# The tail of an encoder layer on one core: last columns' sums added to the residual ahead, last products in two halves, one more block weighed on GpSimd

## The chip, the cores and the metric

The kernel runs on one core of a Trainium2 chip. A core has a matrix engine (TensorE; PE in the profile, with PEld for the loads of its stationary operand), a vector engine (VectorE, DVE), a scalar engine (ScalarE, ACT), a general engine (GpSimd, POOL), a synchronizing engine (SyncE, SP) that issues most transfers, and 16 DMA engines. The metric is the time of one execution on the device in microseconds (us); of several runs the median stands.

## The reference

One layer of a streaming encoder for 256 rows of 2048 columns: a half-step feed-forward part, a pooling and gated linear attention mixer, cross attention on 256 memory tokens, a second half-step feed-forward part, and a last norm. Only the end matters here:

```python
D_MODEL, SEQ, D_FF, RMS_EPS = 2048, 256, 5632, 1e-6

def rms_norm(x, gain):
    y = x * lax.rsqrt(jnp.mean(x * x, axis=-1, keepdims=True) + RMS_EPS)
    return y * gain

def swiglu(h, w_gate, w_up, w_down):
    return (jax.nn.silu(h @ w_gate) * (h @ w_up)) @ w_down

x = x + 0.5 * swiglu(rms_norm(x, ffn2_norm), ffn2_w_gate, ffn2_w_up, ffn2_w_down)
out = rms_norm(x, final_norm)
```

## The kernel before

Matrix products keep fp32 accuracy by splitting each operand into a high and a low part and adding three products: high by high, high by low, low by high (`products`, L357). Activations are the stationary operand, 128x128; weights stream past, 512 columns at a time, into one PSUM bank. The 256 rows are two halves h of 128 rows, here called the first rows (h = 0) and the second rows (h = 1). The 2048 columns are four blocks `nb` of 512; two blocks come with one weight unit (b = 0 for blocks 0 and 1, b = 1 for 2 and 3). Weights pass as units of 1 MB: loaded, split by ScalarE and VectorE, then used (`Stream`, L34); an item that `st.op` adds stands in the program's order behind the unit before it. Instructions are issued from each engine's own queue in order. The order within a queue is the scheduler's, except where `in_order` (L1552) keeps the program's, or `issue_after` sets one instruction behind another.

The end of the kernel is the third part of the last down projection (`down_last` and `down_end`, L1486 and L1502). `block_s` (L514) sums most of its inner dimension. For b = 0 the sums go into the residual x at once. For b = 1 they stay in PSUM (`more=True`), because the last two slices of the inner dimension are added to the same banks later. The last two slices are two more units (`end_unit`, L1522), taken in this order:

1. the first rows of blocks 0 and 1, then 2 and 3. For each block come its six products in `mm` (L1507), then `update` (L1535, VectorE: x += 0.5 * sums), `square` (L1541, ScalarE: squares, with their sum per row into `ss`) and `weigh` (L1546, GpSimd: x times the last gain `gB`, written over the scratch of the squares);
2. `second_half` (L1603): the products of the second rows, blocks 0 to 3, and after them in program order the updates, squares and `weigh` of these, `row_factor` (L1555) for each half, and `finish` (L1585), which multiplies a stretch of columns by the row factor `Rcol` and stores it.

Blocks 0 and 1 of the last slices have fresh banks (`pe` in the profile); blocks 2 and 3 go on in `block_s`'s (`pt`). GpSimd weighs all four blocks of the first rows and blocks 0 and 1 of the second. For blocks 2 and 3 of the second rows `finish` multiplies by factor and gain in one VectorE instruction (L1594). Elsewhere it is a ScalarE scale (L1592) or a VectorE `tensor_scalar_mul` (L1598) of the weighed block. `row_factor` takes the sum of squares (for the second rows: the sum of blocks 0 to 2, made ahead by `three_of_four`, plus block 3's), a square root on ScalarE (L1568), and on VectorE a reciprocal, a Newton step and a reciprocal (L1571 to L1575). Its argument `between` is work put on VectorE between the root's issue and the first reciprocal. There are nine stores to `out`; eight are issued on SP, and one (second rows, blocks 0 and 1, 512 KB) on ScalarE's queue.

Of the kernel before, what the change touches and what calls it, by code (L numbers as in the profile page):

```python
# [15 lines left out]
D = 2048  # L16
# [83 lines left out]
def build(ctx, tc, I, out):  # L100
# [256 lines left out]
    def products(ps, act, k, h, wh, wl, first, last):  # L357

        tok = slice(h * P, (h + 1) * P)
        parts = [(act[:, k, 0, tok], wh), (act[:, k, 0, tok], wl), (act[:, k, 1, tok], wh)]  # L360
        for i, (a, w) in enumerate(parts):
            nc.tensor.matmul(ps, a, w, start=first and i == 0, stop=last and i == 2)  # L362

    def block_t(srcs, act, evict, delays=(0, 0), amid=None):

# [148 lines left out]
    def block_s(srcs, act, sums, order, evict, merge=None, sevens=None, late=0, home=parts_tile,  # L514
                more=False, amid=None, behind=None):

        sevens = [g for g in order if g in (sevens or sums.pairs)]  # L520
        held, seen = {"banks": {}}, set()

        def banks(*names):
            t = ptile(uid("pt"))
            for i, n in enumerate(names):
                held["banks"][n] = t[:, i]
            return t

        def open_whole():
            if "ps" not in held:  # L530
                c = banks("P2", "P4")
                held["ps"] = (banks("P3", "P0"), c)

        def open_parts():
            held["parts"] = (banks("P1", "P6"), banks("P7", "P5"))

        names = {(1, 0): "P2", (1, 1): "P4", (0, 0): "P3", (0, 1): "P0"}

        def unit_s(g):
            def fn(weights):  # L540
                if g == sevens[0]:
                    open_parts()
                open_whole()
                fresh = {f"P{i}" for i in range(1, 8)} - seen
                seen.update(fresh)
                ends = ("P1", "P5", "P6", "P7") if g == sevens[-1] else ()
                if "P1" in fresh:
                    order = ("P1", "P7", "P5", "P6", "P2", "P3", "P4")
                elif merge:
                    order = ("P1", "P2", "P4", "P3", "P5", "P6", "P7")  # L550
                else:
                    order = ("P1", "P2", "P3", "P7", "P5", "P6", "P4")
                seven(held["banks"], act, sums, g, fresh, ends, weights, order)
            return fn

        def unit_p(g):
            def fn(wh, wl):
                open_whole()
                wh, wl = (w.rearrange("p (k j n) -> p k j n", j=2, n=NB) for w in (wh, wl))
                def half(j):  # L560
                    for h in range(2):
                        n = names[j, h]
                        for kk in range(2):
                            products(held["banks"][n], act, 2 * g + kk, h, wh[:, kk, j],
                                     wl[:, kk, j], n not in seen and kk == 0,
                                     g == order[-1] and kk == 1 and not more)
                        seen.add(n)

                before = behind and behind.get(order.index(g))
                with ExitStack() as stack:  # L570
                    for j in (1, 0):
                        if before and j == before[0]:
                            stack.enter_context(tc.issue_after(before[1]().ins))
                        half(j)
            return fn

        def combine():

            e = held["e"] = home()
            a, b = held["parts"]  # L580
            nc.scalar.copy(e[:, 0], a[:, 0])
            nc.vector.tensor_tensor(out=e[:, 3], in0=a[:, 1], in1=e[:, 0], op=ALU.add)
            nc.vector.tensor_tensor(
                out=e[:, 1:3], in0=b, in1=e[:, 3:4].to_broadcast([P, 2, NB]), op=ALU.add
            )
            last = nc.vector.tensor_tensor(out=e[:, 3], in0=b[:, 1], in1=e[:, 1], op=ALU.add)
            if merge is not None:
                merge(e[:, 2:4], e[:, 0:2])
            return None, last

        def join(j):
            if merge is not None:
                evict(j, held["ps"][j])
                return
            e = held["e"][:, 0:2] if j else held["e"][:, 2:4]
            among_weights(lambda: (None, nc.vector.tensor_tensor(
                out=e, in0=held["ps"][j], in1=e, op=ALU.add if j else ALU.subtract
            )))
            evict(j, e)

        for at, g in enumerate(order):
            if g in sevens:
                st.unit(srcs[g], unit_s(g), split_seven)
                if g == sevens[-1]:
                    st.op(combine if merge else clump(lambda: among_weights(combine)), late)
            else:
                st.unit(srcs[g], unit_p(g))
            if at in (amid or {}):
                amid[at]()
        for j in (1, 0):  # L610
            f = lambda j=j: join(j)
            st.op(f if merge else clump(f))
# [889 lines left out]
    def down_end(wd, k0, nk, way):  # L1502
# [4 lines left out]
        def mm(b, k, h, wh, wl):  # L1507

            wh, wl = (w.rearrange("p (k j n) -> p k j n", j=2, n=NB) for w in (wh, wl))
            for j in range(2):  # L1510
                nb = 2 * b + j
                if b == 0 and h == 0:
                    acc_ps[nb] = ptile(uid("pe"))
                for kk in range(2):
                    products(acc_ps[nb][:, h, :], ys, k + kk, h, wh[:, kk, j], wl[:, kk, j],
                             b == 0 and kk == 0, kk == 1)
                if h == 0:
                    update(nb, h)
                    square(nb, h)
                    weigh(nb, h)  # L1520

        def end_unit(b):  # L1522
            def fn(wh, wl):
# [17 lines left out]
        def square(nb, h):  # L1541
            return nc.scalar.activation(
                gained(nb, h), x_cols(nb * NB, NB)[:, h], AF.Square, accum_out=ss[:, h, nb : nb + 1]
            )

        def weigh(nb, h):  # L1546
            nc.gpsimd.tensor_tensor(
                out=gained(nb, h), in0=x_cols(nb * NB, NB)[:, h],
                in1=fin["gB"][:, nb * NB : (nb + 1) * NB], op=ALU.mult,
            )  # L1550
# [4 lines left out]
        def row_factor(h, between=None):  # L1555

            t, r = sums[:, h : h + 1], Rcol[:, h : h + 1]
            v, q = chain[:, 0, h : h + 1], chain[:, 1, h : h + 1]
            if h:
                in_order(nc.vector.tensor_scalar(  # L1560
                    out=v, in0=ss[:, h, 3:4], scalar1=0.25 / D, scalar2=t, op0=ALU.mult, op1=ALU.add
                ))
            else:
                in_order(nc.vector.tensor_reduce(out=t, in_=ss[:, h, :4], axis=AX.X, op=ALU.add))
                in_order(nc.vector.tensor_scalar(
                    out=v, in0=t, scalar1=0.25 / D, scalar2=0.25 * EPS, op0=ALU.mult, op1=ALU.add
                ))
            in_order(nc.scalar.activation(q, v, AF.Sqrt))  # L1568
            if between:
                between()  # L1570
            in_order(nc.vector.reciprocal(out=r, in_=q))  # L1571
            in_order(nc.vector.tensor_scalar(
                out=v, in0=v, scalar1=r, scalar2=q, op0=ALU.mult, op1=ALU.add
            ))
            in_order(nc.vector.reciprocal(out=r, in_=v))  # L1575

        def three_of_four(h):

            t = sums[:, h : h + 1]
            in_order(nc.vector.tensor_reduce(out=t, in_=ss[:, h, :3], axis=AX.X, op=ALU.add))  # L1580
            in_order(nc.vector.tensor_scalar(
                out=t, in0=t, scalar1=0.25 / D, scalar2=0.25 * EPS, op0=ALU.mult, op1=ALU.add
            ))
# [1 line left out]
        def finish(engine, h, at, n, queue=nc.sync):  # L1585
# [4 lines left out]
            x = fin[b, h][:, lo : lo + n]  # L1590
            if engine is nc.scalar:
                in_order(nc.scalar.activation(o, x, AF.Copy, scale=r))  # L1592
            elif h == 1 and at >= 2 * NB:
                in_order(nc.vector.scalar_tensor_tensor(  # L1594
                    out=o, in0=o, scalar=r, in1=fin["gB"][:, at : at + n], op0=ALU.mult, op1=ALU.mult
                ))
# [6 lines left out]
        def second_half():  # L1603
# [5 lines left out]
            weigh(0, 1)  # L1609
            finish(act, 0, 0, NB)  # L1610
            in_order(update(1, 1))
            in_order(square(1, 1))
            weigh(1, 1)
            finish(act, 0, NB, half)
            in_order(update(2, 1))
            in_order(square(2, 1))
            in_order(update(3, 1))
            in_order(square(3, 1))
            three_of_four(1)
            finish(dve, 0, 2 * NB, NB)  # L1620
            row_factor(1, lambda: finish(dve, 0, 3 * NB + half, half))
            finish(act, 0, NB + half, half)
            finish(act, 0, 3 * NB, half)
            finish(dve, 1, 2 * NB, NB)
            finish(act, 1, 0, 2 * NB, nc.scalar)
            finish(dve, 1, 3 * NB, NB)
# [12 lines left out]
                    home=end_parts(b), more=b == 1)  # L1639
        for b in range(2):  # L1640
            st.unit(wwide(wd, b * 2 * NB, k0 + nk - 2, 2)[0], end_unit(b))
        st.op(second_half)

    ffn(I["ffn2_w_gate"][0], I["ffn2_w_up"][0], I["ffn2_w_down"][0], down_last, end=END)
# [71 lines left out]
```

## Time and profile before

| | |
|---|---|
| median of three runs | 2073.61 us (2073.44 to 2073.8) |
| the profiled execution's own time | 2073.65 us |
| its span in the profile | 2071.8 us |
| granted TensorE clock | 0.999 |
| HBM read, written | 417.58 MB, 16.78 MB |

In the profile, times within the span count from its start. A row of a timeline gives start, length, engine, line, operation, what is written and read, and the shape. `x2` at its end means that two such instructions stand together, and the bracket holds the engine's idle time before it and what ended that. A row that groups instructions gives the count, the busy time of the group, the mean of one in ns, and the idle time before them. Matmuls are pipelined, so a matmul's own length is longer than the step from one to the next. GpSimd's spans are rough. Line numbers are those of the kernel before.

### The profile page before, as it was taken

The page shows a single profiled execution, that of the slowest core. Times are in us where ns is not written, and L with a number is a line of the kernel's source. Part 1 is how long each engine was busy: PE and PEld are TensorE (multiplying, and loading weights), DVE is VectorE, ACT ScalarE, POOL GpSimd, SP SyncE. Part 2 cuts the span into 40 slices and gives each one's busy share as a digit, 9 for nine tenths or more (in the row PEclk, how much of TensorE's full clock was granted, in tenths as well). Part 3 has the DMA queues.
Part 4 walks back from the last instruction along what each step waited for, and adds up shares of the span by engine and source line. Part 5 has one row for each costly group of instructions (what it writes and reads, how often), then busy time and mean ns, then how long its engine had stood idle before and what let it go on. Part 6 is the DMA issues. An engine that isn't in the chain of part 4 may idle for free.

```text
span 2071.8 us, 24035 instructions
## 1 busy us (share of the span) xinstructions
PE 2060.3 (99%) x9464; PEld 1714.2 (83%) x9464; DVE 1833.3 (88%) x1706; ACT 1168.7 (56%) x1186; POOL 105.9 (5%) x94
## 2 busy tenths in 40 slices
PE   9999999999999999999999999999999999999998
PEld 7888888888888888888888888888888888888886
DVE  7998899989998778889889877989988999889987
ACT  7655455554554666565755544656554565545554
POOL 0000000000000000000000000000000010000001
PEclk9999999999999999999999999999999999999999
DMA  7666666566666655567755455666576765676664
GB/s 265 205 202 224 242 215 216 184 227 234 227 200 224 231 180 183 164 202 278 228 184 185 162 182 183 203 224 219 171 240 220 240 209 186 223 243 223 209 227 154
DMA packets 122985, 435.91 MB, mean 210 GB/s; under 512 B 9845, under 2 KB 13529, under 8 KB 122489
## 3 DMA queue, kind: packets, MB, share of 16 engines
q1 hardware_dynamic: 122696, 433.86, 63.1%
q8 instruction: 74, 1.21, 0.2%
q10 hardware_dynamic: 176, 0.53, 0.1%
q14 instruction: 39, 0.31, 0.0%
HBM read 417.58 MB, written 16.78 MB: 210 GB/s over the span
## 4 chain that ended last, share of the span: by engine, by line
PE 99%; DMA 0%; DVE 0%; ACT 0%; SPq 0%; issue 0%; DVEq 0%; ACTq 0%
PE pt L362 64%; PE pt L507 30%; PE ph L789 2%; PE pl L1399 1%; PE pv L1436 1%; PE px L800 1%; PE pp L1044 0%; PE pe L362 0%; DMA x<-in_x 0%; PE pa L1072 0%; PE tm L1345 0%; PE po L1209 0%; PE px L726 0%; PE pq L1196 0%; DVE wl L453 0%
## 5 line engine op out<-in xcount | busy, mean ns | idle before, releaser
L362 PE MATMUL pt<-wh,xs 128*128 128x512 f32 x2464 | 790.6, 391 | 0.5 <-ACT xs L236 0.5
L1674 ACT CAST wh<-raw 128x2048 fp32r<-128x2048 f32 x244 | 465.6, 1912 | 231.3 <-PE pt L362 129.6
L453 DVE TENSOR_TENSOR wl<-raw,wh 128x2048 fp32r<-128x2048 f32 (+1 forms) x244 | 519.4, 2137 | 84.5 <-ACT wh L1674 84.3
L362 PEld LDWEIGHTS pt<-wh,xs 128*128 128x128 f32 x2464 | 461.9, 188 | 96.0 <-ACT xs L236 0.7
L489 ACT CAST wh<-T 128x1024 fp32r<-128x1024 f32 x260 | 272.7, 1053 | 377.3 <-DVE T L486 364.6
L362 PE MATMUL pt<-wl,xs 128*128 128x512 f32 x1232 | 480.5, 391 | 0.0
L362 PE MATMUL pt<-wh,ys 128*128 128x512 f32 x1456 | 459.2, 389 | 0.0
L362 PEld LDWEIGHTS pt<-wh,ys 128*128 128x128 f32 x1456 | 273.3, 188 | 56.2
L453 DVE TENSOR_TENSOR wl<-T,wh 128x2048 fp32r<-128x2048 f32 (+1 forms) x130 | 292.1, 2247 | 5.6 <-ACT wh L489 5.2
L362 PE MATMUL pt<-wl,ys 128*128 128x512 f32 x728 | 283.8, 390 | 0.0
L362 PEld LDWEIGHTS pt<-wl,xs 128*128 128x128 f32 x1232 | 231.4, 188 | 47.0 <-DVE wl L280 0.2
L280 DVE TENSOR_TENSOR xl<-raw,xh 128x1536 fp32r<-128x1536 f32 x130 | 227.6, 1750 | 19.5 <-ACT xh L279 19.4
L279 ACT CAST xh<-raw 128x1536 fp32r<-128x1536 f32 x130 | 192.5, 1481 | 65.7 <-PE pt L507 44.0
L486 DVE TENSOR_TENSOR T<-T,raw 128x512 f32<-128x512 f32 x260 | 179.3, 689 | 6.7
L362 PEld LDWEIGHTS pt<-wl,ys 128*128 128x128 f32 x728 | 136.7, 188 | 28.2
L486 DVE TENSOR_TENSOR T<-raw 128x1024 f32<-128x1024 f32 x130 | 158.3, 1217 | 0.5
L457 POOL TENSOR_TENSOR wl<-raw,wh 128x768 fp32r<-128x768 f32 x45 | 84.0, 1867 | 1389.8 <-DVE wl L453 1380.7
L507 PE MATMUL pt<-wh,xs 128*128 128x512 f32 x392 | 152.3, 389 | 0.0
L507 PE MATMUL pt<-xh,xs 128*128 128x512 f32 x408 | 151.9, 389 | 0.0
L507 PE MATMUL pt<-wh,xe 128*128 128x512 f32 x320 | 124.3, 389 | 0.0
L507 PEld LDWEIGHTS pt<-xh,xs 128*128 128x128 f32 x408 | 76.6, 188 | 15.9
L507 PEld LDWEIGHTS pt<-wh,xs 128*128 128x128 f32 x392 | 73.6, 188 | 15.2
(270 smaller groups left out, 2054.8 us busy)
## 6 DMA issues: line engine op xcount, KB each, us to landing
raw<-in_ffn_w_down SPq DMA_DIRECT2D x88, 1024.0 KB, 5.7
raw<-in_ffn_w_up SPq DMA_DIRECT2D x80, 1024.0 KB, 5.0
raw<-in_ffn_w_gate SPq DMA_DIRECT2D x77, 1024.0 KB, 5.1
raw<-in_w_in SPq DMA_DIRECT2D x32, 1024.0 KB, 5.1
raw<-in_xattn_w_kv SPq DMA_DIRECT2D x32, 1024.0 KB, 5.1
raw<-in_w_out SPq DMA_DIRECT2D x16, 1024.0 KB, 6.4
raw<-in_xattn_w_q SPq DMA_DIRECT2D x16, 1024.0 KB, 5.6
raw<-in_xattn_w_o SPq DMA_DIRECT2D x16, 1024.0 KB, 5.7
```

What stands on the lines that cost most here:

```text
L279: in_turn("scalar", lambda: nc.scalar.copy(hi, src))
L280: in_turn("vector", lambda: nc.vector.tensor_tensor(out=lo, in0=src, in1=f32(hi), op=ALU.subtract))
L362: nc.tensor.matmul(ps, a, w, start=first and i == 0, stop=last and i == 2)
L453: in_turn("vector", lambda: nc.vector.tensor_tensor(out=lo[:, :n], in0=src[:, :n], in1=f32(hi[:, :n]), op=ALU.subtract))
L457: rest = nc.gpsimd.tensor_tensor(out=lo[:, n:], in0=src[:, n:], in1=f32(hi[:, n:]), op=ALU.subtract)
L486: in_turn("vector", lambda: nc.vector.tensor_tensor(out=o, in0=a, in1=b, op=ALU.add))
L489: in_turn("scalar", lambda: nc.scalar.copy(th[:, c], t[:, c]))
L507: nc.tensor.matmul(banks[n], x, w, start=n in fresh and j == 0, stop=n in ends and j == 2)
L789: rows["turned"] = nc.tensor.transpose(v[:, i, h * P : (h + 1) * P], g[:, h, i * P : (i + 1) * P], ident)
L800: nc.tensor.transpose(v[:, j, h * P : (h + 1) * P], x[:, h, j * P : (j + 1) * P], ident)
L1399: nc.tensor.matmul(ps[:, t, :M], ys[:, 4 * h + d, a, tok], xa["K", h][:, d, b, :], start=i == 0, stop=i == 11,)
L1674: in_turn("scalar", lambda: nc.scalar.copy(hi, raw))
```

## The change

- `block_s` ends the accumulation of the last block's second rows (block 3, h = 1) with its own last product, although the other banks go on.
- Behind the unit of blocks 0 and 1, `update(3, 1)` adds these sums to the residual; it stood behind the last product before.
- The last slices' products for block 3 of the second rows are twelve of 256 columns instead of six of 512. They go into the first halves of the banks that held blocks 0 and 1 of the first rows. `issue_after` puts them behind the product before.
- Their update, square and sum of squares follow in two halves (`last_update`, `last_square`); `ss` has one more column, and the sum made ahead (`all_but_last`) takes four columns instead of three.
- GpSimd weighs block 2 of the second rows too, so that its `finish` is a `tensor_scalar_mul`; only block 3 keeps the instruction with factor and gain.
- First rows: block 2 is scaled and stored right behind `update(1, 1)`; columns 1792 to 2047 behind the last update, ahead of the sums; columns 1536 to 1791 move from ScalarE to VectorE, between root and reciprocal.

```diff
     def products(ps, act, k, h, wh, wl, first, last):
         for i, (a, w) in enumerate(parts):
-            nc.tensor.matmul(ps, a, w, start=first and i == 0, stop=last and i == 2)
+            latest["product"] = nc.tensor.matmul(
+                ps, a, w, start=first and i == 0, stop=last and i == 2
+            )
...
-                                     g == order[-1] and kk == 1 and not more)
+                                     g == order[-1] and kk == 1 and (not more or j == h == 1))
...
+                if (nb, h) == (3, 1):
+                    with tc.issue_after(latest["product"].ins):
+                        for i in range(2):
+                            for kk in range(2):
+                                products(last_part(i), ys, k + kk, h, wh[:, kk, j, columns(i)],
+                                         wl[:, kk, j, columns(i)], kk == 0, kk == 1)
+                    continue
...
+        def columns(i):
+            return slice(i * NB // 2, (i + 1) * NB // 2)
+
+        def last_part(i):
+            return acc_ps[i][:, 0, : NB // 2]
...
+        def last_update(i):
+            xn = x_cols(3 * NB, NB)[:, 1, columns(i)]
+            return nc.vector.scalar_tensor_tensor(
+                out=xn, in0=last_part(i), scalar=0.5, in1=xn, op0=ALU.mult, op1=ALU.add
+            )
+
+        def last_square(i):
+            return nc.scalar.activation(
+                gained(3, 1)[:, columns(i)], x_cols(3 * NB, NB)[:, 1, columns(i)], AF.Square,
+                accum_out=ss[:, 1, 3 + i : 4 + i],
+            )
...
-                    out=v, in0=ss[:, h, 3:4], scalar1=0.25 / D, scalar2=t, op0=ALU.mult, op1=ALU.add
+                    out=v, in0=ss[:, h, 4:5], scalar1=0.25 / D, scalar2=t, op0=ALU.mult, op1=ALU.add
...
-        def three_of_four(h):
+        def all_but_last(h):
...
-            in_order(nc.vector.tensor_reduce(out=t, in_=ss[:, h, :3], axis=AX.X, op=ALU.add))
+            in_order(nc.vector.tensor_reduce(out=t, in_=ss[:, h, :4], axis=AX.X, op=ALU.add))
...
-            elif h == 1 and at >= 2 * NB:
+            elif h == 1 and at >= 3 * NB:
...
             finish(act, 0, 0, NB)
             in_order(update(1, 1))
+            finish(dve, 0, 2 * NB, NB)
             in_order(square(1, 1))
             weigh(1, 1)
             finish(act, 0, NB, half)
             in_order(update(2, 1))
             in_order(square(2, 1))
-            in_order(update(3, 1))
-            in_order(square(3, 1))
-            three_of_four(1)
-            finish(dve, 0, 2 * NB, NB)
-            row_factor(1, lambda: finish(dve, 0, 3 * NB + half, half))
+            weigh(2, 1)
+            in_order(last_update(0))
+            in_order(last_square(0))
+            in_order(last_update(1))
+            in_order(last_square(1))
+            finish(dve, 0, 3 * NB + half, half)
+            all_but_last(1)
+            row_factor(1, lambda: finish(dve, 0, 3 * NB, half))
             finish(act, 0, NB + half, half)
-            finish(act, 0, 3 * NB, half)
             finish(dve, 1, 2 * NB, NB)
             finish(act, 1, 0, 2 * NB, nc.scalar)
             finish(dve, 1, 3 * NB, NB)
...
             st.unit(wwide(wd, b * 2 * NB, k0 + nk - 2, 2)[0], end_unit(b))
+            if b == 0:
+                st.op(lambda: update(3, 1))
         st.op(second_half)
```

## The prediction

> **What bounds the kernel now.** First the page: its span, its busy table, the shares of its chain of waits, and the product's group (count, busy us, mean ns).
>
> ```profile
> span 2071.8 us, 24035 instructions
> PE 2060.3 (99%) x9464; PEld 1714.2 (83%) x9464; DVE 1833.3 (88%) x1706; ACT 1168.7 (56%) x1186; POOL 105.9 (5%) x94
> PE 99%; DMA 0%; DVE 0%; ACT 0%; SPq 0%; issue 0%; DVEq 0%; ACTq 0%
> ...
> L362 PE MATMUL pt<-wh,ys 128*128 128x512 f32 x1456 | 459.2, 389 | 0.0
> ```
>
> TensorE is busy 2060.3 of 2071.8 us and is 99% of the chain; the change takes no product away. What it can move lies behind the last product. There the chain in order of time reads (start, length, what):
>
> ```profile
> 2060.49 2.73 PE pt L362 x12
> 2063.25 0.70 DVE x L1537
> 2063.98 0.73 ACT O L1542 x2
> 2064.73 0.21 DVE chain L1560
> ...
> 2065.22 0.17 DVE Rcol L1571
> ...
> 2065.72 0.17 DVE Rcol L1575
> 2065.92 0.75 DVE x L1594
> ```
>
> The last product ends at 2063.22. Update of the last 512 columns, square and sum, and a few small steps give the row factor of the second 128 rows ("factor" below) at 2065.89. All of those rows, 1 MB, can only be scaled and stored after it. The queue issues (timeline), the windows of the whole core (DMA share and GB/s last) and SP's waits show the rest:
>
> ```profile
> 2066.70 0.35 SPq L1599 DMA_DIRECT2D out<-x  x1
> 2067.16 0.38 ACTq L1599 DMA_DIRECT2D out<-x  x1
> 2067.36 0.33 SPq L1599 DMA_DIRECT2D out<-x  x1
> 2065.20:2067.50 2.30, 0.00 (x0) 0.00 (x0) 2.02 (x6) 1.93 (x3) 0.00 (x0) 0.66 0.81 283
> 2067.50:2070.40 2.90, 0.00 (x0) 0.00 (x0) 0.00 (x0) 0.00 (x0) 0.00 (x0) 0.50 0.95 363
> SPq L1703 <- DMA out<-x: 3.0, 1, 3.0
> ```
>
> The three stores of the second rows (256, 512, 256 KB) pass in one stretch, 2067.5 to 2070.4, at a DMA share of 0.95: 1.05 MB at 363 GB/s is 2.9 us. So the end hangs on when the factor is known and when the first of these stores is issued, then on throughput. From the data's end the span has 1.4 us left, which nothing here touches. The profiled execution took 2073.65 us, 1.85 more than its span; the median of the runs, 2073.61, is 0.04 less. I sum against the former and carry the difference to the median.
>
> **The products.** Six products of 512 columns become twelve of 256. Twelve of 512 took 2.73 us, 0.227 each. Products with 256 columns stand elsewhere (timeline; groups by form, for the product and its weight load)
>
> ```profile
> 1293.03 3.04 PE L1436 MATMUL pv<-PT,V 128*128 128x256 f32 x24
> ...
> L1436 PE MATMUL pv<-PT,V 128*128 128x256 f32 x96 | 12.4, 282 | 0.0
> L1436 PEld LDWEIGHTS pv<-PT,V 128*128 128x128 f32 x96 | 12.3, 191 | 0.5
> ```
>
> One takes 0.28, so the 24 start 2.76 / 23 = 0.120 apart, closer than their weight loads last. The six that go start at 2061.69 (2063.22 less 0.39 of the last and five steps of 0.227), and the twelve then end at 2061.69 + 11 x 0.120 + 0.28 = 2063.29 instead of 2063.22: 0.07 lost, and the first half is ready at 2062.57. Bounds: nothing lost, if they stream at half of 0.227; 0.8 lost, if each took a whole weight load of 0.19. The row decides for 0.07. The banks they write were read long before (the first 512 columns' update of the first rows), so no wait is added on TensorE.
>
> **The early update of the last columns**, 512 wide on VectorE, goes behind the second update of the first rows. VectorE idles there:
>
> ```profile
> 2056.68 0.69 DVE L1537 SCALAR_TENSOR_TENSOR x<-pt,x 128x512 f32<-128x512 f32 x1 [0.89 <-PE pt L362]
> ```
>
> One update fits into 0.89, so it costs 0. Without that cover the update behind it comes up to 0.69 late, and this reaches the end only through the first rows' factor.
>
> **The halves behind the products.** Widths cost as follows (groups of lines by form):
>
> ```profile
> L767 DVE SCALAR_TENSOR_TENSOR x<-pt,x 128x1024 f32<-128x1024 f32 x30 | 36.1, 1215 | 0.0
> L1537 DVE SCALAR_TENSOR_TENSOR x<-pe,x 128x512 f32<-128x512 f32 x4 | 2.7, 684 | 3.2 <-PE pe L362 3.2
> L1592 ACT ACTIVATE x<-O,Rcol 128x256 f32<-128x256 f32 x3 | 1.4, 492 | 0.0
> L1592 ACT ACTIVATE x<-O,Rcol 128x1024 f32<-128x1024 f32 x1 | 1.1, 1148 | 0.0
> L1598 DVE TENSOR_SCALAR x<-O,Rcol 128x256 f32<-128x256 f32 x1 | 0.3, 344 | 0.0
> ```
>
> An update is 1.04 ns a column: 256 of them take 0.42. ScalarE's step is 0.85 ns: a square of 256 with its read takes 0.51 instead of 0.73. Were VectorE free, the second half's update would run 2063.32 to 2063.74, its square to 2064.28 behind the first's, and the sum would be taken at 2064.31 instead of 2064.73: 0.42 gained. That is what the split could give.
>
> **The rows scaled sooner, and GpSimd.** But VectorE isn't free. Columns 1024 to 1535 of the first rows are now scaled right behind the update that ends at 2061.40, and GpSimd weighs at that time:
>
> ```profile
> 2060.73 0.67 DVE L1537 SCALAR_TENSOR_TENSOR x<-pe,x 128x512 f32<-128x512 f32 x1
> 2061.07 1.30 POOL L1547 TENSOR_TENSOR O<-x,gB 128x512 f32<-128x512 f32 x1 [0.32 <-ACT O L1542]
> 2062.32 1.30 POOL L1547 TENSOR_TENSOR O<-x,gB 128x512 f32<-128x512 f32 x1
> 2062.06 0.19 ACT L1542 ACTIVATION_READ_ACCUMULATOR O<-x 128x1 f32 x1
> 2061.89 0.69 DVE L1537 SCALAR_TENSOR_TENSOR x<-pt,x 128x512 f32<-128x512 f32 x1 [0.49 <-PE pt L362]
> 2062.62 0.64 ACT L1542 ACTIVATE O<-x 128x512 f32<-128x512 f32 x1
> 2063.16 0.18 ACT L1542 ACTIVATION_READ_ACCUMULATOR O<-x 128x1 f32 x1
> 2064.11 0.47 DVE L1598 TENSOR_SCALAR x<-O,Rcol 128x512 f32<-128x512 f32 x1
> ```
>
> By duration the scaling would fit: 0.47 into a gap of 0.49. In the kernel before, it ran at 2064.11, with GpSimd done at 2063.62. What it does beside a GpSimd instruction another place shows (timeline, and the instructions of one line with their minimum, median and maximum in ns):
>
> ```profile
> 799.92 1.91 DVE L1185 TENSOR_SCALAR m<-kq,F 128x64 f32<-128x64 f32 x1
> 799.92 1.86 POOL L457 TENSOR_TENSOR wl<-raw,wh 128x768 fp32r<-128x768 f32 x1 [6.04 <-DVE wl L453]
> L1185 DVE TENSOR_SCALAR m<-kq,F x12: 240/243/1910, 788.6 to 802.1; 128x64 f32<-128x64 f32 x12
> 837.45 0.71 DVE L1015 TENSOR_TENSOR s<-u 128x542 f32<-128x542 f32 x1
> 837.66 2.22 POOL L457 TENSOR_TENSOR wl<-raw,wh 128x768 fp32r<-128x768 f32 x1 [27.10 <-DVE wl L453]
> ```
>
> The same operation from SBUF to SBUF took 243 ns at the median, and 1910 where GpSimd had just begun: it ended 0.05 behind GpSimd's end. The other way round GpSimd waited too: 2.22 instead of 1.86, with VectorE ahead until 838.16. The updates, which read PSUM and one SBUF tensor, kept their 0.69 beside GpSimd.
>
> So, step by step. The early scaling starts at 2061.33 and is held to GpSimd's end at 2062.37; its 512 columns at 0.51 ns ((475 - 344) / 256) end at 2062.65. Queued behind it on VectorE are the update of columns 1024 to 1535, which before started at 2061.89, and with it everything of the last columns. That update now runs 2062.57 to 2063.26 (consecutive VectorE instructions overlap by 0.08), the halves to 2063.60 and 2063.94. The products' 0.07 is hidden by this. ScalarE waits for these: its square of the third block ends at 2064.01, the halves' at 2064.43 and 2064.85, and the sum is taken at 2064.88: 0.15 late instead of 0.42 early.
>
> GpSimd's second block, pushed behind the scaling, runs 2062.65 to about 2063.9. The scaling of columns 1792 to 2047 comes at 2063.86 and ends about 2064.2; GpSimd's third and new block, ready at 2064.09 (0.08 behind its square), runs 2064.2 to between 2065.36 and 2065.5. The scaling of columns 1536 to 1791, which moves from ScalarE into VectorE's wait for the square root, comes at 2065.01, is held to that end, and ends 0.15 after it. The reciprocal behind it, before at 2065.22, starts between 2065.43 and 2065.57. The factor is late by 0.21 to 0.35; I take 0.25, since the held block of GpSimd ran somewhat under its free length behind VectorE (1.72 of 1.86).
>
> **Behind the factor.** The second rows' columns 1024 to 1535 are scaled with GpSimd's weighed block: 0.47 instead of 0.75, so the first store is issued 0.28 sooner. GpSimd's work for it is done by then. ScalarE, relieved of one block of 256, starts its 1024 columns at once (0.07 sooner), and the last store follows 0.33 sooner. The stretch is limited by throughput from the first store on, so I take 0.28, with 0.07 and 0.33 as bounds. The stores stay nine and each occupies its queue 0.33 to 0.38. Those of the first rows leave SP sooner, past queues that are idle: 0 on the path, and up to 0.3 more gained if their tail (0.81 share in the window before 2067.5) held up the second rows'.
>
> **The sum:** 0.25 late for the factor, less 0.28: -0.03. The time is 2073.6, no change.
>
> The Trainium skill, "SBUF — State Buffer", section "Who interferes with whom", says that VectorE in a two-port mode, which tensor_scalar can enter, and GpSimd exclude each other for the whole instruction, and that the order of issue decides. The 1910 ns above agree; whether a waiting VectorE goes ahead of GpSimd's next block no run here shows, and by the page it would, which is the case summed.
>
> **The rivals.**
>
> *Nothing is held.* The scaling fits its gap. For it: the rows of the updates beside GpSimd. Against it: 1910 against 243. The factor comes 0.42 sooner, the stores another 0.28: -0.70, 2072.9. Chance 0.10.
>
> *The second scaling loses its race.* The 256 columns at 2063.86 come only 0.2 ahead of GpSimd's third block. If GpSimd goes first (2064.09 to 2065.37), the scaling ends at 2065.52, the two small steps behind it at 2065.8, the sum and the root follow, and the reciprocal starts at 2066.3: 1.08 late, less 0.28: +0.8, 2074.4. Decided by 0.2 us in the order of starts. Chance 0.15.
>
> *GpSimd keeps the interface for its second block*, the case on the other side. That block waits only for a square that ended at 2062.25, so it can follow at 2062.32 without a pause, and the early scaling ends at 2063.90. The update of the third block runs to 2064.51, the halves to 2064.86 and 2065.21, their squares to 2066.10, the sum is at 2066.13, and the scaling before the reciprocal is held by the third block to 2066.75. The reciprocal is 1.45 late, less 0.28: +1.17, 2074.8. For it: back-to-back blocks at 2061.07 and 2062.32. Against it: a request that has waited since 2061.33. It decides from GpSimd's first end at 2062.37. Chance 0.20.
>
> *The change doesn't halve the products.* If weight loads set the pace, the twelve end at 2064.04 and the scaling behind them meets the third block as in the second rival: +0.8. Against it the 0.120 of the row. With whatever I haven't seen, 0.05.
>
> The case summed has the remaining 0.50.
>
> **How the numbers follow.** The likeliest gives 2073.6; its own range, from the bounds of its costs (factor 0.15 to 0.35 late, stores 0.07 to 0.6 gained), is 2073.1 to 2073.9. The range goes from the first rival, 2072.9, less 0.2 for scatter of the runs (2073.44 to 2073.8), to the third, 2074.8, plus 0.2: 2072.7 to 2075.0. About 0.2% (4.1 us) is what a measurement can tell from no change here; no case comes near it, since what follows the last product is 8.6 us in all and half of that is transfer and end. So same 0.97; faster 0.01; slower 0.02.
>
> **What would show it.** Right: a scaling of 512 columns on VectorE of about 1.3 us that ends within 0.3 of a GpSimd end near 2062.4; the third update starting near 2062.6; the reciprocal of the second rows near 2065.5; 256-column products 0.12 apart; stores of the second rows half a microsecond behind the factor. Wrong: that scaling at 0.47 (first rival), one of over 2 us (third), or a 256-column scaling of over 1 us at 2063.9 (second). A TensorE gap before 2061 would overturn the whole sum.

## The result, and the profile after

The changed kernel is slower: 2076.88 us (median of 21 runs, 2076.06 to 2077.5) against 2073.69 (median of 21, 2073.06 to 2074.66), 3.19 us or 0.15%. The ratio is 1.0014 with a 95% interval of 1.0009 to 1.002. The forecast was 2073.6, no change, within 2072.7 to 2075.0.

The page of the changed kernel, its span and busy table:

```profile
span 2075.5 us, 24056 instructions
PE 2060.7 (99%) x9470; PEld 1714.9 (83%) x9470; DVE 1835.1 (88%) x1709; ACT 1168.5 (56%) x1187; POOL 107.2 (5%) x95
```

TensorE is busy 0.4 us more than before and the span is 3.7 longer, so the loss isn't TensorE's. Its chain of waits at the end (start, length, what):

```profile
2060.92 1.36 PE pt L362 x6
2062.28 0.73 PE pe L362 x6
2063.03 0.69 DVE x L1552
...
2064.81 1.31 DVE x L1625
2066.11 0.61 DVE x L1552
2066.75 0.72 ACT O L1557 x2
...
2068.35 0.21 DVE chain L1587
...
2069.38 0.17 DVE Rcol L1602
...
2069.64 0.48 DVE x L1625
2070.13 0.68 DVE x L1621
```

Before, the chain stayed on TensorE to its last product. Here it leaves after the sixth of the twelve last products, for an `update` of 512 columns (L1552) from a `pe` tile. VectorE's timeline shows which one; the bracket is its idle time and what ended it:

```profile
2052.60 0.39 PE L362 MATMUL pe<-wh,ys 128*128 128x512 f32 x1
2059.91 0.16 DVE L1592 TENSOR_SCALAR chain<-sums 128x1 f32<-128x1 f32 x1
2063.03 0.69 DVE L1552 SCALAR_TENSOR_TENSOR x<-pe,x 128x512 f32<-128x512 f32 x1 [2.96 <-PE pe L362]
2063.64 0.15 DVE L1598 RECIPROCAL Rcol<-chain 128x1 f32<-128x1 f32 x1
```

And the same place before:

```profile
2052.17 0.39 PE L362 MATMUL pe<-wh,ys 128*128 128x512 f32 x1
2059.49 0.15 DVE L1565 TENSOR_SCALAR chain<-sums 128x1 f32<-128x1 f32 x1
2059.56 0.68 DVE L1537 SCALAR_TENSOR_TENSOR x<-pe,x 128x512 f32<-128x512 f32 x1
```

The first products of the last units stand at 2052.17 before and 2052.60 after; over the runs below they lie between 2051.58 and 2053.00. Times are therefore counted from that product from here on ("at 7.39"). What follows it took 2071.8 - 2052.17 = 19.6 us before and 2075.5 - 2052.60 = 22.9 after: 3.3, which accounts for the loss of 3.19.

The update of block 0 of the second rows started at 7.39 before and at 10.43 after: 3.04 late. The products it needs had ended at 2059.56, more than 3 us earlier. What it waited for is the first half of block 3's last products. A PSUM tile here is two banks, one for the first rows of a block and one for the second. The halves write the first-row bank of the tile `pe` whose second-row bank the update reads. Queued behind it on VectorE stood the small steps of the first rows' factor, the updates of blocks 1, 2 and 3, and all scalings.

### The profile page after: what moved, and what is told of

Its sections match the earlier page's. It is cut to its first block, busy times and chain, and to the rows that moved or that the text cites. A ratio compares the mean times of both kernels' runs of the same rounds, so it can differ in the third digit from the quotient of the medians.

```text
span 2075.5 us, 24056 instructions
## 1 busy us (share of the span) xinstructions
PE 2060.7 (99%) x9470; PEld 1714.9 (83%) x9470; DVE 1835.1 (88%) x1709; ACT 1168.5 (56%) x1187; POOL 107.2 (5%) x95
## 4 chain that ended last, share of the span: by engine, by line
PE 99%; DVE 0%; DMA 0%; ACT 0%; issue 0%; SPq 0%; DVEq 0%; ACTq 0%
PE pt L362 64%; PE pt L509 30%; PE ph L791 2%; PE pl L1401 1%; PE pv L1438 1%; PE px L802 1%; PE pe L362 0%; PE pp L1046 0%; DMA x<-in_x 0%; PE pa L1074 0%; PE tm L1347 0%; PE po L1211 0%; PE px L728 0%; PE pq L1198 0%; DVE wl L455 0%
## 5 line engine op out<-in xcount | busy, mean ns | idle before, releaser
L280 DVE TENSOR_TENSOR xl<-raw,xh 128x1536 fp32r<-128x1536 f32 x130 | 227.6, 1751 | 19.5 <-ACT xh L279 19.4
```

What stands on the lines that cost most here:

```text
L280: in_turn("vector", lambda: nc.vector.tensor_tensor(out=lo, in0=src, in1=f32(hi), op=ALU.subtract))
```

## The experiments

The theory: an update waits for the last product that the program lists ahead of it into the same PSUM tile, whichever bank of the tile is written. First rival: VectorE waits for a batch of TensorE's products, because of `issue_after` or of how products signal. Second rival: the loss comes from the scaling held beside GpSimd. "Stretch" is the time from the first product of the last units to the end of the span. The median of the kernel before on the same chip stands beside each median. The ratio and its 95% interval are estimated over all runs and need not equal the quotient of the two medians.

### The last products listed behind the updates

`mm` keeps the operands, and the products are listed in `second_half`, still under `issue_after`. The order on TensorE and VectorE doesn't change.

```diff
                 if (nb, h) == (3, 1):
-                    with tc.issue_after(latest["product"].ins):
...
+                    fin["last"] = (k, wh[:, :, j], wl[:, :, j])
                     continue
...
             in_order(update(1, 1))
+            last_products()
             finish(dve, 0, 2 * NB, NB)
```

> The changed kernel with one thing moved: the twelve last products stand in the program behind the updates of blocks 0 and 1 of the second rows; TensorE's own order is the same. Tile theory (an update waits for the last product that the program puts ahead of it into the same PSUM tile, whichever bank): the first update of the second rows no longer waits for the first half of the last products; it starts about 7.4 us behind the first product of the last units (10.4 in the changed kernel, 7.4 before). The stretch from that first product to the end of the span is 19.6 us (before 19.6, changed 22.9), and the time is within 0.3 of the kernel before. Signal theory (VectorE waits for a batch of TensorE's products, because of the order set with issue_after, wherever they go): the update still starts at 10.4, the stretch stays at 22.9. Theory that the loss comes from the scaling held beside GpSimd: the stretch stays near 22, since that scaling is as before.

Measured: 2073.99 us against 2073.86, ratio 1.0001 (0.9993 to 1.001); stretch 2072.2 - 2052.35 = 19.9. VectorE's and GpSimd's timeline:

```profile
2052.35 0.39 PE L362 MATMUL pe<-wh,ys 128*128 128x512 f32 x1
2059.73 0.68 DVE L1556 SCALAR_TENSOR_TENSOR x<-pe,x 128x512 f32<-128x512 f32 x1
2061.25 1.30 POOL L1578 TENSOR_TENSOR O<-x,gB 128x512 f32<-128x512 f32 x1 [0.44 <-ACT O L1561]
2061.50 1.34 DVE L1629 TENSOR_SCALAR x<-O,Rcol 128x512 f32<-128x512 f32 x1
2062.50 1.48 POOL L1578 TENSOR_TENSOR O<-x,gB 128x512 f32<-128x512 f32 x1
2062.76 0.68 DVE L1556 SCALAR_TENSOR_TENSOR x<-pt,x 128x512 f32<-128x512 f32 x1
2063.36 0.74 DVE L1567 SCALAR_TENSOR_TENSOR x<-pe,x 128x256 f32<-128x256 f32 x2
2065.08 0.21 DVE L1591 TENSOR_SCALAR chain<-ss,sums 128x1 f32<-128x1 f32 x1
2065.61 0.15 DVE L1602 RECIPROCAL Rcol<-chain 128x1 f32<-128x1 f32 x1
2066.10 0.16 DVE L1606 RECIPROCAL Rcol<-chain 128x1 f32<-128x1 f32 x1
2066.88 0.33 SPq L1630 DMA_DIRECT2D out<-x  x1
```

The update is back at 7.38, and the 3 us are gone, with the held scaling still there (1.34). At this end of the kernel TensorE and VectorE do the same instructions in the same order as in the changed kernel. So the wait isn't the chip's: it comes into the program with the place at which a product is listed. Both rivals fall: `issue_after` is still there, and so is the held scaling.

### The halves in other tiles

```diff
         def last_part(i):
-            return acc_ps[i][:, 0, : NB // 2]
+            return acc_ps[2 + i][:, 0, : NB // 2]
```

> The changed kernel with the two halves written to the first-row banks of blocks 2 and 3 instead of blocks 0 and 1; the order in the program is not touched. Tile theory: the updates of blocks 0 and 1 come in time (7.4 us behind the first product), and now the update of block 2 waits for the first half (10.4 us behind the first product instead of 9.7), which the held scaling does to it anyway: stretch 19.6 to 19.8. Signal theory: the first update at 10.4, stretch 22.9.

Measured: 2074.25 against 2073.86, ratio 0.9999 (0.999 to 1.0008); stretch 2071.6 - 2051.93 = 19.7.

```profile
2051.93 0.39 PE L362 MATMUL pe<-wh,ys 128*128 128x512 f32 x1
2059.31 0.68 DVE L1552 SCALAR_TENSOR_TENSOR x<-pe,x 128x512 f32<-128x512 f32 x1
2062.36 0.69 DVE L1552 SCALAR_TENSOR_TENSOR x<-pt,x 128x512 f32<-128x512 f32 x1
```

Update 0 comes at 7.38, with the program's order untouched: the wait goes with the tile. That it passed to block 2's update (10.43) fits, but doesn't show it, since the held scaling ends at about that time.

### The wait alone, and the same products without it

The kernel before with the early update, and the last six products whole in the first-row bank of block 0, or (second run) of block 3.

```diff
+                if (nb, h) == (3, 1):
+                    with tc.issue_after(latest["product"].ins):
+                        for kk in range(2):
+                            products(acc_ps[0][:, 0, :], ys, k + kk, h, wh[:, kk, j], wl[:, kk, j],
+                                     kk == 0, kk == 1)
+                    continue
...
-            in_order(update(3, 1))
+            in_order(last_update())
...
+            if b == 0:
+                st.op(lambda: update(3, 1))
```

> The kernel before with the early update and the last six products, whole (512 columns), written to the first-row bank of block 0; no halves, no row moved, no block more on GpSimd. Tile theory: the first update of the second rows waits for all of them, 11.05 us behind the first product, and with it the rest: stretch 22.5, time about 2.9 above the kernel before. Theory of the held scaling: nothing is scaled early here, so 19.6 and no loss.

> As the run with the wait alone, but the six products go to the first-row bank of block 3, whose tile no update reads between. Tile theory: no wait, stretch 19.6, time within 0.2 of the kernel before. Signal theory: as with the other bank, 22.5.

Measured in block 0's tile: 2076.97 against 2073.86, ratio 1.0014 (1.0005 to 1.0024); stretch 22.8.

```profile
2052.17 0.39 PE L362 MATMUL pe<-wh,ys 128*128 128x512 f32 x1
2063.25 0.69 DVE L1545 SCALAR_TENSOR_TENSOR x<-pe,x 128x512 f32<-128x512 f32 x1 [3.61 <-PE pe L362]
```

In block 3's: 2073.93 against 2073.86, ratio 1.0 (0.9991 to 1.0008); stretch 19.9.

```profile
2051.58 0.39 PE L362 MATMUL pe<-wh,ys 128*128 128x512 f32 x1
2058.96 0.68 DVE L1545 SCALAR_TENSOR_TENSOR x<-pe,x 128x512 f32<-128x512 f32 x1
2062.66 0.69 DVE L1551 SCALAR_TENSOR_TENSOR x<-pt,x 128x512 f32<-128x512 f32 x1 [0.67 <-PE pt L362]
```

Without halves, moved rows or a block more on GpSimd the wait alone makes 3.1 us: the update waits for all six products, to 11.08. Another tile, with the same listing and the same `issue_after`, takes it away. The early update as such costs nothing that these runs can tell.

### The scaling alone

```diff
             in_order(update(1, 1))
+            finish(dve, 0, 2 * NB, NB)
             in_order(square(1, 1))
...
             three_of_four(1)
-            finish(dve, 0, 2 * NB, NB)
```

> The kernel before with only the scaling of columns 1024 to 1535 of the first rows set behind the update of block 1. Held scaling: it takes 1.3 (0.47 before) and the update of block 2 starts at 10.4 instead of 9.72, but the update of block 3 waits for TensorE until 11.08 anyway, so reciprocal at 13.0 and no change in time; stretch 19.5 to 19.9. If the scaling is not held: 0.47 and block 2 at 9.72. The rival that the changed kernel's loss comes from this scaling wants about 3 us more here.

Measured: 2073.57 against 2073.75, ratio 0.9996 (0.9987 to 1.0005); stretch 2072.0 - 2052.32 = 19.7.

```profile
2061.47 1.34 DVE L1598 TENSOR_SCALAR x<-O,Rcol 128x512 f32<-128x512 f32 x1
2062.73 1.36 DVE L1537 SCALAR_TENSOR_TENSOR x<-pt,x 128x512 f32<-128x512 f32 x2
```

It is held, and block 2's update starts at 10.41, but block 3's follows it without idle time (x2) and ends where it did before: a hold of 0.87 that is fully covered by the wait for TensorE. The second rival wanted 3 us more here, and they don't come.

### The halves alone, and the scaling ahead of GpSimd

Both list the last products late, as in the first run, and leave rows and GpSimd's blocks as before. The second sets the scaling ahead of `update(1, 1)`; the marked lines are where it differs from the first.

```diff
+            finish(dve, 0, 2 * NB, NB)
             in_order(update(1, 1))
             last_products()
...
             all_but_last(1)
-            finish(dve, 0, 2 * NB, NB)
```

> The early update and the two halves alone, with the last products behind the updates in the program (no wait on the tile); rows and GpSimd as in the kernel before. Times count from the first product of the last units. Sum of the prediction without a held scaling: second half updated at 11.15 to 11.57, sum of squares of the second half at 12.11; the scaling of 512 columns that stands between (0.47) then sets the sum, at about 12.35 instead of 12.56, and the reciprocal comes at 12.85 instead of 13.04. Last store 14.99 instead of 15.19, stretch 19.4 (before 19.6 to 19.9). If the halves bring nothing, 19.6 to 19.9. The time is within 0.3 of the kernel before, below what the rounds tell apart.

> As the halves alone, and the scaling of columns 1024 to 1535 set ahead of the update of block 1, right behind the first rows' factor (8.64), where GpSimd starts only at 8.90. If the order of issue decides, it takes 0.47 and GpSimd waits about 0.2; the update of block 1 ends at 9.65 and block 2 still starts at 9.72. With nothing left between, the sum comes at 12.15 and the reciprocal at 12.65 instead of 13.04; last store 14.8 instead of 15.19, stretch 19.2 to 19.5. If GpSimd takes the interface anyway, the scaling takes over 1.3 and the gain is lost.

Measured, halves alone: 2074.35 against 2073.75, ratio 1.0002 (0.9993 to 1.0011); stretch 20.3. VectorE, the last store, and SP's wait for the stores at the end:

```profile
2053.00 0.39 PE L362 MATMUL pe<-wh,ys 128*128 128x512 f32 x1
2064.15 0.42 DVE L1567 SCALAR_TENSOR_TENSOR x<-pe,x 128x256 f32<-128x256 f32 x1 [0.29 <-PE pe L362]
2065.26 0.21 DVE L1591 TENSOR_SCALAR chain<-ss,sums 128x1 f32<-128x1 f32 x1
2067.88 0.33 SPq L1630 DMA_DIRECT2D out<-x  x1
SPq L1739 <- DMA out<-x: 3.9, 1, 3.9
```

The sum comes at 12.26, 0.3 earlier than before, and the last store at 14.88 instead of 15.19, both about 0.1 sooner than expected. The stretch is a miss: SP's last wait was 3.9 instead of 3.0, and from the last store's issue to the end it took 5.4 us instead of 4.4. The eight other profiles have 4.4 to 4.7 for this. The execution profiled here was the slowest of the eleven (2075.11), so its end may not be the usual one.

Scaling ahead: 2073.81 against 2073.75, ratio 0.9999 (0.999 to 1.0008); stretch 2071.6 - 2051.83 = 19.8, again above the expected 19.2 to 19.5.

```profile
2060.58 0.49 DVE L1629 TENSOR_SCALAR x<-O,Rcol 128x512 f32<-128x512 f32 x1
2060.73 1.50 POOL L1578 TENSOR_TENSOR O<-x,gB 128x512 f32<-128x512 f32 x1 [0.44 <-ACT O L1561]
2063.87 0.16 DVE L1611 TENSOR_REDUCE sums<-ss 128x1 f32<-128x4 f32 x1 [0.46 <-ACT O L1572]
```

With VectorE first by 0.15 the scaling takes 0.49 and GpSimd 1.50: the order of starts decides who waits. But the update behind it, and with it ScalarE's squares, came later, and the sum made ahead waited 0.46 for them. The reciprocal came at 12.98 where 12.65 was expected, and the last store at 15.12 where 14.8 was: this is a miss too. None of these versions is faster than the kernel before by what the runs can tell.

## Why the prediction was wrong

The step that failed is in the part on the products: "The banks they write were read long before (the first 512 columns' update of the first rows), so no wait is added on TensorE." That is right for TensorE: the halves started without a gap. It asked only who must have read a bank before it is written. It didn't ask who reads the tile afterwards, in the order in which the program lists things. `second_half` lists all products first and the updates after them, so the updates of blocks 0 and 1 come behind products that write another bank of their tiles. The wait was added on VectorE, for a value that the update doesn't use. It was in the diff (`acc_ps[i]` in `last_part`). The last units of the kernel before show no such wait: there no other product into a tile stands between a block's own products and its update. No rival named it: the case on the other side was a hold beside GpSimd. None of the signs named for being wrong appeared either: in the changed kernel the early scaling took 1.31 and the first 256-column one 0.34, as forecast. Only the times at which they ran were 3 us late.

The other steps can be read from the run with the products listed late, which differs from the changed kernel by this wait alone. Predicted times are less 2052.17.

- Products: 0.07 lost, 0.120 apart. Measured: the last one ended at 11.11 instead of 11.05, and they start 0.119 apart. Right.
- Early update at no cost, behind the second update of the first rows, in an idle time of 0.89. The cost is right, by the run with whole products in block 3's tile. The place is wrong, as the rows below the list show: the scheduler put it ahead of all four updates of the first rows, into a wait of 2.56 us. That this gap was there too was luck.
- Held scaling: from 9.16 to 10.48, the third update at 10.40, GpSimd's second block done at about 11.7. Measured: 9.15 to 10.49, 10.41, 11.63. Right, and VectorE, which was waiting, went ahead of GpSimd's next block, whose 1.30 became 1.48. The Trainium skill's "SBUF — State Buffer", section "Who interferes with whom", has the order of issue decide; these runs agree.
- Sum at 12.71, reciprocal between 13.26 and 13.40. Measured: 12.73 and 13.26. The second reciprocal, which ends the factor, started at 13.75 against 13.55 before: 0.20 late where 0.25 was taken.
- Behind the factor: the first store 0.28 sooner. Measured: issued at 14.53, 0.78 behind the start of the second reciprocal, against 0.98 before: 0.20. Loss and gain cancel, as the sum had it, but both were smaller than taken, by 0.05 and 0.08, so that they cancel is luck in part. The last store was issued at 15.19, as before, and the stretch differs from before's by 0.2, within what the end scatters.

VectorE's timeline around the early update, changed kernel (two rows) and before:

```profile
2051.52 0.68 DVE L1552 SCALAR_TENSOR_TENSOR x<-pt,x 128x512 f32<-128x512 f32 x1
2054.16 0.69 DVE L1552 SCALAR_TENSOR_TENSOR x<-pe,x 128x512 f32<-128x512 f32 x1 [1.96 <-PE pe L362]
2053.73 0.69 DVE L1537 SCALAR_TENSOR_TENSOR x<-pe,x 128x512 f32<-128x512 f32 x1 [2.56 <-PE pe L362]
```

In the changed kernel the wait is 3.04, the held scaling and what follows bring the factor to 3.23 late (2069.55 against 2065.89, each from its first product), and the stretch is 3.3 longer. So 3.0 of the 3.2 us are the missed wait. As this wait moves all of VectorE's queue, there was nothing to hide it: the updates, which used to run beside the last products, came after them.

What stays open is a gain of some tenths from the halves: with the halves alone the sum was 0.3 sooner (the 0.42 of the prediction's free case shows in no run), but the end of the stores scatters by more than that, and the median didn't show it. The prediction also held that less than 0.2% can't be told from no change. The 0.15% here can, with an interval of 1.0009 to 1.002 from 21 runs each.

## What to carry to other kernels

When a product is sent to a free part of a buffer that others still read, look in program order for every later reader of the whole tile, not only for readers of the part written: it may wait for a write that it has no use for. Price that wait by everything that is queued behind the reader on its own engine. Listing the write behind those readers, or choosing a tile without later readers, took it away here at no cost that the runs can tell; and it is worth checking such an edit by the first idle time that is new on any engine.

## What was not expected of the hardware

From the issue of the last store to the end of the span, profiles with the same three last stores took 4.4 to 5.4 us (2067.36 to 2071.8 before, 2067.88 to 2073.3 with the halves alone). Gains of a few tenths ahead of the stores can't be seen in the time of single runs of this kernel. Single runs can mislead by more: on the chip of the last three experiments, two of 27 runs of the kernel before took 2076.84 and 2077.29, as long as the changed kernel. What made them long is open.
